# Second product of a ConvGLU as seven block products over all of K, with resident weights

## The chip, the cores and the metric

One core of one Trainium2 chip runs the kernel. The metric is the device time of one execution in microseconds; lower is better. Five engines work side by side and are told apart in the profile: TensorE (PE, its weight loads PEld), VectorE (DVE), ScalarE (ACT), GpSimd (POOL), and SyncE (SP), whose queue issues nearly all of the transfers.

## The reference

A causal decoder trunk of two layers over 1024 positions of width 1024: a hybrid attention layer and a latent attention layer, each followed by a gated MLP (ConvGLU) and a gated per-layer embedding (`ple`). The change concerns the MLP, which is the same in both layers:

```python
def conv_glu(hn, w_in, conv_w, conv_b, w_out):
    u, gate_in = jnp.split(hn @ w_in, 2, axis=-1)
    c = (conv_w[0] * shift_right(gate_in, 2) + conv_w[1] * shift_right(gate_in, 1)
         + conv_w[2] * gate_in + conv_b)
    return (jax.nn.gelu(c, approximate=False) * u) @ w_out
...
h = h + conv_glu(rmsnorm(h, ffn_norm[i]), ffn_w_in[i], ffn_conv_w[i], ffn_conv_b[i], ffn_w_out[i])
```

Everything is in 32-bit floats.

## The kernel before, in words

Activations lie transposed: features on the 128 partitions (tiles of 128, `KD` = 8 for the width, `NFT` = 22 for the MLP), positions along the free dimension in two blocks of 512 (`BW`). A product keeps 32-bit accuracy by splitting each operand into a high part and a rest (`split`, L199 to L203: ScalarE casts the high part, L202; GpSimd or VectorE subtracts it from the operand, L203) and multiplying three times, high by high, high by rest and rest by high (`mm3`, L221 to L228). So every block product is three matmuls of 128x512 for each tile of K, all of them recorded at L228.

`conv_glu` (L515) has two phases, called once per layer.

The first, `ffn_in` (L619), makes the gated activations. It already uses a seven-product scheme: for a pair of feature tiles, a 2x2 block product (two halves of K by two output tiles, two halves of K by two position blocks) is made from seven products of sums and differences of blocks (`seven`, L418; for the first pair `seven_first`, L480) where the plain way takes eight. `pair(i)` (L634) makes the four gate blocks, convolves them (`conv`, L645), makes the four up blocks, multiplies them by the gate (`up`, L656 to L661) and stores each of the four results `u` to `md` in device memory, one DMA of 256 KB each (L661). The weights pass through a ring of eight raw tiles (`raw`) and are summed on GpSimd and split on GpSimd and VectorE (`seven_weights`, L387). The seven operands of the phase are made beforehand; two of them lie in the ring of block tiles `mh`/`ml` (`block_tile`, L352, eight of each), five in a pool `x7`.

The second, `ffn_out` (L694), multiplies the activations by `w_out`, 2816 to 1024, in the plain way. `h` was put away in `hs` during the start of the MLP and is first reloaded, 16 blocks of 256 KB (L525 to L528). Then K is taken in eleven groups of two tiles. For a group the activations are loaded (`mraw`, L705) and split into `mh`/`ml`, the weights loaded (`wraw`, three buffers) and split into `whi`/`wlo` (six buffers), and for each of the 8 output tiles and 2 position blocks six matmuls go into a bank of PSUM, which VectorE then adds into `h`:

```python
for f in range(KD):
    for b in range(NBLK):
        ps = pm.tile([P, BW], F32, name="mm")
        self.mm3(ps, [((w[f // 4][0][:, f % 4], w[f // 4][1][:, f % 4]), (mh[b], ml[b]))
                      for w, (mh, ml) in zip(ws, ms)])
        nc.vector.tensor_tensor(out=h[:, f, bs], in0=h[:, f, bs], in1=ps, op=OP.add)
```

PSUM has eight banks for these products. After the MLP `ple` (L719) loads `praw`, splits it, multiplies it, norms and splits all of `h`, and multiplies again.

The kernel is written as a sequence of tile operations; the order of each engine's instructions is set by a scheduler at build time, which may put an operation ahead of others that stand before it in the text. Each engine then takes its instructions strictly in that order, and SP its transfers in its own. Memory is given out by pools: a tile that takes the place of an earlier one waits until that one has been read for the last time.

Of the kernel before, what the change touches and what calls it, by code (L numbers as in the profile page):

```python
# [11 lines left out]
F32 = mybir.dt.float32  # L12
R = mybir.dt.float32r
# [7 lines left out]
P = 128  # L21
S = 1024
# [100 lines left out]
class Trunk:  # L123
# [391 lines left out]
    def conv_glu(self, h, layer, c_h, c_raw, start):  # L515

        nc, tc, t = self.nc, self.tc, self.t
        md = [tc.dram_tile([P, S], F32, name=f"md{layer}_{i}") for i in range(NFT)]
        hs = start[0]
        with ExitStack() as ctx:  # L520
            self.ffn_in(ctx, h, layer, c_h, md, start[1])
        c_raw.close()
        pool = Lines(c_h.enter_context(tc.tile_pool(reuse_waits="tile", name=f"h2_{layer}", bufs=1, side="right")))
        h = Rows([pool.tile([P, 2, S], F32, name=f"h2_{k}") for k in range(0, KD, 2)])
        for k in range(KD):  # L525
            for b in range(NBLK):
                bs = slice(b * BW, (b + 1) * BW)
                nc.sync.dma_start(out=h[:, k, bs], in_=hs[:, k, bs])  # L528
        with ExitStack() as ctx:
            self.ffn_out(ctx, h, layer, md)  # L530
        return h
# [87 lines left out]
    def ffn_in(self, ctx, h, layer, c_h, md, operands):  # L619
# [14 lines left out]
        def pair(i):  # L634
# [5 lines left out]
            cs = [[None, None], [None, None]]  # L640

# [14 lines left out]
            def up(m, b):  # L656
                def ev(ps, add):
                    u = ep.tile([P, BW], F32, name="u", bufs=4)
                    nc.vector.tensor_tensor(out=u, in0=ps, in1=add, op=OP.add)
                    nc.vector.tensor_tensor(out=u, in0=u, in1=cs[m][b], op=OP.mult)  # L660
                    nc.sync.dma_start(out=md[tiles[m]][:, b * BW:(b + 1) * BW], in_=u)  # L661
                return ev

            outs = lambda f: [[f(m, b) for b in range(2)] for m in range(2)]
            if i == 0:
# [14 lines left out]
                for _ in ups:  # L680
                    pass
                return
# [5 lines left out]
            for _ in self.seven(ep, xs, weights(tiles), outs(up)):  # L688
                pass

# [3 lines left out]
    def ffn_out(self, ctx, h, layer, md):  # L694
        nc, tc, t = self.nc, self.tc, self.t
        wp, pm = self.wp, self.pm
        mp = Lines(ctx.enter_context(tc.tile_pool(reuse_waits="tile", name="mraw", bufs=6)))
        group = 2
        for c in range(NFT // group):
            ms, ws = [], []  # L700
            for i in range(c * group, (c + 1) * group):
                mh, ml = [[self.block_tile(j, R) for b in range(NBLK)] for j in range(2)]
                for b in range(NBLK):
                    raw = mp.tile([P, BW], F32, name="mraw")
                    nc.sync.dma_start(out=raw, in_=md[i][:, b * BW:(b + 1) * BW])  # L705
                    self.split(mh[b], ml[b], raw, eng=None if c else nc.vector)
                ms.append((mh, ml))
                src = t["ffn_w_out"][layer, i * P:(i + 1) * P, :].rearrange("p (f m) -> p f m", m=P)
                ws.append([self.weights(wp, src[:, f:f + 4], 4, P) for f in (0, 4)])
            for f in range(KD):  # L710
                for b in range(NBLK):
                    bs = slice(b * BW, (b + 1) * BW)
                    ps = pm.tile([P, BW], F32, name="mm")
                    self.mm3(ps, [((w[f // 4][0][:, f % 4], w[f // 4][1][:, f % 4]), (mh[b], ml[b]))
                                  for w, (mh, ml) in zip(ws, ms)])
                    nc.vector.tensor_tensor(out=h[:, f, bs], in0=h[:, f, bs], in1=ps, op=OP.add)  # L716
# [1150 lines left out]
def layout(inputs):  # L1867
# [6 lines left out]
    a["ffn_w_out"] = g["ffn_w_out"]  # L1874
# [71 lines left out]
```

## Time and profile before

| | us |
|---|---|
| median of 3 runs | 3014.35 |
| lowest and highest run | 3010.39, 3021.18 |
| the profiled execution, its own time | 3004.87 |
| its span, first to last instruction | 3003.2 |

The profile is of one execution. Busy time of an engine is the time in which at least one of its instructions runs; matmuls overlap, so their spacing and not their duration tells what one costs. In a row of a group, the number after the bar is the mean duration in ns, and after the second bar stands the idle time of the engine before those instructions, with what ended it. In a window's row the clock is the granted one, as a share of full speed.

### The profile page before, as it was taken

Reading aid. Unit: us, or ns where it says so; the run is one execution under the profiler, and the core shown is the slowest. Engines: PE = TensorE matmul, PEld = TensorE weight load, DVE = VectorE, ACT = ScalarE, POOL = GpSimd, SP = SyncE. Lnnn points to the kernel's source line nnn. Section 1 sums busy time; section 2 is a strip of 40 time slices with the busy share of each in tenths; the row PEclk is TensorE's granted clock in tenths of the full one; section 3 lists DMA queues with packets and bytes.
Section 4 is the critical chain, followed back from the end, with each engine's and each line's share of the span. In section 5 each row is a group of like instructions: output and inputs, shape, how many; then the busy total and the mean of one; then the engine's idle time right before and its main releaser. Section 6 shows DMA issues by size and latency. Waiting matters only on the chain.

```text
span 3003.2 us, 40819 instructions
## 1 busy us (share of the span) xinstructions
PE 2884.8 (96%) x14542; PEld 2234.5 (74%) x14542; DVE 2082.0 (69%) x3202; ACT 1259.8 (42%) x2277; POOL 1038.2 (35%) x804
## 2 busy tenths in 40 slices
PE   8999999999899999999998899999989999999997
PEld 6777777677678888888886656566758888878886
DVE  7766657875787777655798677776497777655577
ACT  6424436562343333312644434344344333422274
POOL 4332420103544444544232500010434444454323
PEclk9999989999999999999999899999989999999998
DMA  4344565635122222532121300013212222343111
GB/s 142 111 148 130 153 202 153 162 96 179 39 75 84 85 85 71 200 102 78 50 90 57 111 19 24 18 41 105 76 48 88 81 84 85 111 167 95 55 58 57
DMA packets 221020, 286.10 MB, mean 95 GB/s; under 512 B 62256, under 2 KB 106800, under 8 KB 220816
## 3 DMA queue, kind: packets, MB, share of 16 engines
q1 hardware_dynamic: 215632, 272.99, 29.3%
q10 hardware_dynamic: 5184, 10.49, 1.0%
q8 instruction: 115, 1.88, 0.3%
q14 instruction: 89, 0.73, 0.1%
HBM read 200.50 MB, written 81.79 MB: 94 GB/s over the span
## 4 chain that ended last, share of the span: by engine, by line
PE 81%; DVE 11%; issue 4%; ACT 2%; POOL 1%; DMA 1%; SPq 0%; DVEq 0%; ACTq 0%; POOLq 0%
PE mm L228 60%; PE o L1024 3%; PE s L1035 2%; PE o L1772 1%; PE tr L1760 1%; PE s L1038 1%; PE mm L995 1%; PE s L1039 1%; PE z L1744 1%; PE z L1741 1%; DVE itmp L1481 1%; PE pk L1452 1%; DVE xinv L1483 1%; DVE x L203 1%; PE mm L1059 1%
## 5 line engine op out<-in xcount | busy, mean ns | idle before, releaser
L228 PE MATMUL mm<-x,whi 128*128 128x512 f32 x1760 | 555.8, 396 | 27.0 <-DVE x L203 14.5
L203 POOL TENSOR_TENSOR wlo<-wraw,whi 128x512 fp32r<-128x512 f32 (+2 forms) x238 | 317.4, 1341 | 570.7 <-ACT whi L202 524.9
L228 PE MATMUL mm<-mh,whi 128*128 128x512 f32 x1056 | 412.9, 391 | 4.5 <-DVE h L716 4.5
L228 PEld LDWEIGHTS mm<-x,whi 128*128 128x128 f32 x1760 | 335.2, 191 | 108.4 <-DVE x L203 22.0
L228 PE MATMUL mm<-ml,whi 128*128 128x512 f32 x1056 | 413.5, 392 | 1.6 <-DVE ml L203 1.4
L228 PE MATMUL mm<-mh,wlo 128*128 128x512 f32 x1056 | 412.3, 390 | 0.0
L228 PE MATMUL mm<-xh,whi 128*128 128x512 f32 (+1 forms) x1016 | 404.8, 398 | 6.6 <-ACT xh L208 6.5
L228 PE MATMUL mm<-xh,wlo 128*128 128x512 f32 (+1 forms) x1016 | 397.3, 391 | 1.2 <-POOL wlo L203 1.2
L716 DVE TENSOR_TENSOR h<-h,mm 128x512 f32<-128x512 f32 x352 | 241.6, 687 | 220.4 <-PE mm L228 199.0
L228 PE MATMUL mm<-xl,whi 128*128 128x512 f32 (+1 forms) x1016 | 390.6, 392 | 0.5 <-DVE xl L209 0.5
L228 PE MATMUL mm<-x,wlo 128*128 128x512 f32 x880 | 346.0, 395 | 1.1 <-DVE wlo L203 1.1
L202 ACT CAST whi<-raw 128x512 fp32r<-128x512 f32 x268 | 166.3, 621 | 347.0 <-PE mm L228 305.4
L202 ACT CAST whi<-wraw 128x512 fp32r<-128x512 f32 (+2 forms) x242 | 143.0, 595 | 326.1 <-issue 147.3
L203 POOL TENSOR_TENSOR wlo<-raw,whi 128x512 fp32r<-128x512 f32 x108 | 160.7, 1489 | 301.6 <-ACT whi L202 287.1
L228 PEld LDWEIGHTS mm<-mh,whi 128*128 128x128 f32 x1056 | 199.1, 189 | 47.4 <-DVE h L716 5.4
L228 PEld LDWEIGHTS mm<-ml,whi 128*128 128x128 f32 x1056 | 199.0, 188 | 45.4 <-DVE ml L203 3.1
L228 PEld LDWEIGHTS mm<-xh,whi 128*128 128x128 f32 x1016 | 194.7, 192 | 50.7 <-ACT xh L208 7.3
L228 PEld LDWEIGHTS mm<-mh,wlo 128*128 128x128 f32 x1056 | 198.9, 188 | 41.5 <-issue 0.5
L228 PEld LDWEIGHTS mm<-xl,whi 128*128 128x128 f32 x1016 | 194.3, 191 | 44.5 <-issue 4.8
L228 PEld LDWEIGHTS mm<-xh,wlo 128*128 128x128 f32 x1016 | 194.3, 191 | 42.3 <-POOL wlo L203 2.1
L228 PEld LDWEIGHTS mm<-x,wlo 128*128 128x128 f32 x880 | 168.5, 191 | 37.2 <-DVE wlo L203 2.6
L1041 ACT ACTIVATE w<-s 128x512 f32<-128x512 f32 (+1 forms) x192 | 94.1, 491 | 166.8 <-PE s L1039 149.3
(418 smaller groups left out, 5269.0 us busy)
## 6 DMA issues: line engine op xcount, KB each, us to landing
raw<-in_ffn_w_in SPq DMA_DIRECT2D x176, 256.0 KB
wraw<-in_ffn_w_out SPq DMA_DIRECT2D x88, 256.0 KB
md<-u SPq DMA_DIRECT2D x88, 256.0 KB
mraw<-md SPq DMA_DIRECT2D x88, 256.0 KB
wraw<-in_hyb_w_in SPq DMA_DIRECT2D x52, 256.0 KB
hs<-h SPq DMA_DIRECT2D x32, 256.0 KB
h<-hs SPq DMA_DIRECT2D x32, 256.0 KB
wraw<-in_ple_w_gate SPq DMA_DIRECT2D x32, 256.0 KB
```

What stands on the lines that cost most here:

```text
L202: nc.scalar.copy(out=hi, in_=src)
L203: (eng or nc.gpsimd).tensor_tensor(out=lo, in0=src, in1=hi, op=OP.subtract)
L228: nc.tensor.matmul(ps, lhsT=w, rhs=x, start=first and i == 0, stop=last and i == len(seq) - 1)
L716: nc.vector.tensor_tensor(out=h[:, f, bs], in0=h[:, f, bs], in1=ps, op=OP.add)
L995: nc.tensor.matmul(ps[:, :n], lhsT=qh[e][0:96, i * P:(i + 1) * P], rhs=kh[ki[e]][0:96, c * BW:c * BW + n], start=True, stop=True)
L1024: nc.tensor.matmul(op_[64 * e:64 * e + 64, off:], lhsT=v[:, j, vc:vc + 64], rhs=ws[e][:, :n], start=j == 0, stop=j == nj - 1)
L1035: nc.tensor.matmul(s[:, :n], lhsT=kh[ki[e]][0:97, js], rhs=qh[e][0:97, qs], start=True, stop=False)
L1038: nc.tensor.matmul(s[:, :n], lhsT=kh[ki[e]][0:96, js], rhs=ql[e][0:96, qs], start=False, stop=False)
L1039: nc.tensor.matmul(s[:, :n], lhsT=kl[ki[e]][0:96, js], rhs=qh[e][0:96, qs], start=False, stop=True)
L1041: nc.scalar.activation(out=w[:, :n], in_=s[:, :n], func=AF.Exp, scale=MLA_SCALE)
L1059: nc.tensor.matmul(den[64 * e:64 * e + 64], lhsT=self.ones[:, :64], rhs=acc[e], start=True, stop=True)
L1452: nc.tensor.matmul(ps[:, c], lhsT=bk[rows, c0 + c, e:e + 2].rearrange("p a t -> p (a t)"), rhs=ar[rows, :, ts], start=True, stop=True)
```

## The change

`ffn_out` makes its product in the manner of `ffn_in`: K is halved by taking the two tiles of a pair as the two halves, the 1024 output features are halved into even and odd tiles, the positions into the two blocks. Each of seven jobs runs over all eleven pairs (`N`) and sums the product of one operand block and one weight block in four PSUM banks (`Q` = 4 output tiles); 33 matmuls go into each bank. The activations' seven operands are made in the first phase: three are blocks as they are (jobs 0, 1, 6), four are sums and differences, made in place on VectorE at the end of each pair (`combine`), and all seven are stored to `md`. The raw weights stay in memory for the whole phase, 44 tiles `a` of 256 KB, and GpSimd sums them in place, job after job. In a step, the operand block is loaded (into a `wraw` buffer) and split on ScalarE and VectorE, and the job's weight block is split on ScalarE and, in jobs 0 to 2, GpSimd, later VectorE. At the end of a job ScalarE copies (jobs 0, 2, 3) or VectorE adds the four banks into quarters of `h`; after jobs 3, 4 and 5 the kept `h` is loaded from `hs` through three buffers (`kept`) and added, in place of the reload at the start. `layout` brings `w_out` into the order of the blocks on the host.

```diff
@@ -515,19 +515,16 @@
     def conv_glu(self, h, layer, c_h, c_raw, start):
         nc, tc, t = self.nc, self.tc, self.t
-        md = [tc.dram_tile([P, S], F32, name=f"md{layer}_{i}") for i in range(NFT)]
+        md = [[tc.dram_tile([P, BW], F32, name=f"md{layer}_{n}_{i}") for i in range(NFT // 2)] for n in range(7)]
         hs = start[0]
         with ExitStack() as ctx:
             self.ffn_in(ctx, h, layer, c_h, md, start[1])
         c_raw.close()
         pool = Lines(c_h.enter_context(tc.tile_pool(reuse_waits="tile", name=f"h2_{layer}", bufs=1, side="right")))
         h = Rows([pool.tile([P, 2, S], F32, name=f"h2_{k}") for k in range(0, KD, 2)])
-        for k in range(KD):
-            for b in range(NBLK):
-                bs = slice(b * BW, (b + 1) * BW)
-                nc.sync.dma_start(out=h[:, k, bs], in_=hs[:, k, bs])
         with ExitStack() as ctx:
-            self.ffn_out(ctx, h, layer, md)
+            self.ffn_out(ctx, h, hs, layer, md)
         return h
     def ffn_start(self, h, layer):
@@ -638,6 +635,23 @@
                 gts.append(ep.tile([P, 2 + S], F32, name=f"gt{m}"))
                 nc.vector.memset(gts[m][:, 0:2], 0.0)
             cs = [[None, None], [None, None]]
+            us = {}
+            def store(n, x):
+                nc.sync.dma_start(out=md[n][i], in_=x)
+            def combine():
+                tt = nc.vector.tensor_tensor
+                b11, b12, b21, b22 = us[0, 0], us[0, 1], us[1, 0], us[1, 1]
+                tt(out=b22, in0=b22, in1=b12, op=OP.subtract)
+                store(5, b22)
+                tt(out=b12, in0=b12, in1=b11, op=OP.subtract)
+                store(3, b12)
+                tt(out=b11, in0=b22, in1=b11, op=OP.add)
+                store(4, b11)
+                tt(out=b21, in0=b21, in1=b11, op=OP.subtract)
+                store(2, b21)
             def gate(m, b):
                 return lambda ps, add: nc.vector.tensor_tensor(out=gts[m][:, 2 + b * BW:2 + (b + 1) * BW], in0=ps, in1=add, op=OP.add)
@@ -658,7 +672,10 @@
                     u = ep.tile([P, BW], F32, name="u", bufs=4)
                     nc.vector.tensor_tensor(out=u, in0=ps, in1=add, op=OP.add)
                     nc.vector.tensor_tensor(out=u, in0=u, in1=cs[m][b], op=OP.mult)
-                    nc.sync.dma_start(out=md[tiles[m]][:, b * BW:(b + 1) * BW], in_=u)
+                    us[m, b] = u
+                    n = {(0, 0): 0, (1, 0): 1, (1, 1): 6}.get((m, b))
+                    if n is not None:
+                        store(n, u)
                 return ev
             outs = lambda f: [[f(m, b) for b in range(2)] for m in range(2)]
@@ -679,6 +696,7 @@
                 conv(1, 1)
                 for _ in ups:
                     pass
+                combine()
                 return
             for _ in self.seven(ep, xs, weights([NFT + f for f in tiles]), outs(gate)):
                 pass
@@ -687,33 +705,83 @@
                     conv(m, b)
             for _ in self.seven(ep, xs, weights(tiles), outs(up)):
                 pass
+            combine()
         for i in range(NFT // 2):
             pair(i)
-    def ffn_out(self, ctx, h, layer, md):
+    def ffn_out(self, ctx, h, hs, layer, md):
         nc, tc, t = self.nc, self.tc, self.t
         wp, pm = self.wp, self.pm
-        mp = Lines(ctx.enter_context(tc.tile_pool(reuse_waits="tile", name="mraw", bufs=6)))
-        group = 2
-        for c in range(NFT // group):
-            ms, ws = [], []
-            for i in range(c * group, (c + 1) * group):
-                mh, ml = [[self.block_tile(j, R) for b in range(NBLK)] for j in range(2)]
-                for b in range(NBLK):
-                    raw = mp.tile([P, BW], F32, name="mraw")
-                    nc.sync.dma_start(out=raw, in_=md[i][:, b * BW:(b + 1) * BW])
-                    self.split(mh[b], ml[b], raw, eng=None if c else nc.vector)
-                ms.append((mh, ml))
-                src = t["ffn_w_out"][layer, i * P:(i + 1) * P, :].rearrange("p (f m) -> p f m", m=P)
-                ws.append([self.weights(wp, src[:, f:f + 4], 4, P) for f in (0, 4)])
-            for f in range(KD):
-                for b in range(NBLK):
-                    bs = slice(b * BW, (b + 1) * BW)
-                    ps = pm.tile([P, BW], F32, name="mm")
-                    self.mm3(ps, [((w[f // 4][0][:, f % 4], w[f // 4][1][:, f % 4]), (mh[b], ml[b]))
-                                  for w, (mh, ml) in zip(ws, ms)])
-                    nc.vector.tensor_tensor(out=h[:, f, bs], in0=h[:, f, bs], in1=ps, op=OP.add)
+        Q, N = KD // 2, NFT // 2
+        lo, hi = slice(0, BW), slice(BW, S)
+        ap = Lines(ctx.enter_context(tc.tile_pool(reuse_waits="tile", name="wout", bufs=1)))
+        kp = Lines(ctx.enter_context(tc.tile_pool(reuse_waits="tile", name="kept", bufs=3)))
+        a = [[[ap.tile([P, Q, P], F32, name=f"a{m}{k}_{i}") for k in range(2)] for m in range(2)] for i in range(N)]
+        add = lambda out, x, y: nc.vector.tensor_tensor(out=out, in0=x, in1=y, op=OP.add)
+        def load(m, k):
+            def at(i):
+                nc.sync.dma_start(out=a[i][m][k], in_=t["ffn_w_out"][layer, i, k, m])
+                return a[i][m][k]
+            return at
+        def sums(m, k, one, two, op):
+            def at(i):
+                nc.gpsimd.tensor_tensor(out=a[i][m][k], in0=a[i][one[0]][one[1]], in1=a[i][two[0]][two[1]], op=op)
+                return a[i][m][k]
+            return at
+        def s1(i):
+            load(1, 0)(i)
+            return sums(1, 0, (1, 0), (1, 1), OP.add)(i)
+        jobs = [load(0, 0), load(0, 1), load(1, 1), s1, sums(0, 0, (1, 0), (0, 0), OP.subtract),
+                sums(1, 1, (1, 1), (0, 0), OP.subtract), sums(0, 1, (0, 1), (0, 0), OP.subtract)]
+        def kept(f, bs):
+            x = kp.tile([P, BW], F32, name="kept")
+            nc.sync.dma_start(out=x, in_=hs[:, f, bs])
+            add(h[:, f, bs], h[:, f, bs], x)
+        for n, weight in enumerate(jobs):
+            ps = [pm.tile([P, BW], F32, name="mm") for q in range(Q)]
+            for i in range(N):
+                raw = wp.tile([P, BW], F32, name="wraw", bufs=self.wbufs[0])
+                nc.sync.dma_start(out=raw, in_=md[n][i])
+                xh, xl = [self.block_tile(j, R) for j in range(2)]
+                self.split(xh, xl, raw, eng=nc.vector)
+                wh, wl = [wp.tile([P, Q, P], R, name="w" + x, bufs=self.wbufs[1]) for x in ("hi", "lo")]
+                self.split(wh, wl, weight(i), eng=nc.vector if n > 2 else nc.gpsimd)
+                for q in range(Q):
+                    self.mm3(ps[q], [((wh[:, q], wl[:, q]), (xh, xl))], first=i == 0, last=i == N - 1)
+            for q in range(Q):
+                h00, h01, h10, h11 = [h[:, 2 * q + m, bs] for m in range(2) for bs in (lo, hi)]
+                if n == 0:
+                    nc.scalar.copy(out=h01, in_=ps[q])
+                elif n == 1:
+                    add(h00, ps[q], h01)
+                elif n == 2:
+                    nc.scalar.copy(out=h10, in_=ps[q])
+                elif n == 3:
+                    nc.scalar.copy(out=h11, in_=ps[q])
+                    kept(2 * q, lo)
+                elif n == 4:
+                    add(h01, ps[q], h01)
+                    add(h10, h10, h01)
+                    add(h11, h11, h01)
+                    nc.vector.tensor_copy(out=h01, in_=h11)
+                    kept(2 * q, hi)
+                elif n == 5:
+                    add(h10, ps[q], h10)
+                    add(h11, ps[q], h11)
+                    kept(2 * q + 1, lo)
+                    kept(2 * q + 1, hi)
+                else:
+                    add(h01, ps[q], h01)
     def ple(self, h, layer, last=(None, None), cuts=()):
@@ -1871,7 +1939,8 @@
     a["x"] = np.ascontiguousarray(g["x"][0].T.reshape(KD, P, S).transpose(1, 0, 2))
     a["p"] = np.ascontiguousarray(g["p"][:, 0].transpose(0, 2, 1).reshape(2, 2, P, S).transpose(0, 2, 1, 3))
     a["ffn_w_in"] = np.stack([_blocks(w) for w in g["ffn_w_in"]])
-    a["ffn_w_out"] = g["ffn_w_out"]
+    a["ffn_w_out"] = np.ascontiguousarray(g["ffn_w_out"].reshape(2, NFT // 2, 2, P, KD // 2, 2, P).transpose(0, 1, 2, 5, 3, 4, 6))
     a["ple_w_proj"] = np.stack([_blocks(w) for w in g["ple_w_proj"]])
     a["ple_w_gate"] = np.stack([_blocks(w) for w in g["ple_w_gate"]])
     cols = np.zeros((P, NCOLS), np.float32)
```

## Rows read from the trace of the kernel before

**Rows 1.** The page, part 1 (busy us by engine) and part 2 (busy tenths, clock).
```profile
PE 2884.8 (96%) x14542; PEld 2234.5 (74%) x14542; DVE 2082.0 (69%) x3202; ACT 1259.8 (42%) x2277; POOL 1038.2 (35%) x804
...
PE   8999999999899999999998899999989999999997
...
PEclk9999989999999999999999899999989999999998
```

**Rows 2.** Windows: length, PE, PEld, DVE, ACT, POOL busy us (instructions), clock, DMA share, GB/s.
```profile
860.00:1210.00 350.00, 350.00 (x1546) 289.82 (x1545) 250.13 (x354) 139.52 (x225) 159.35 (x109) 1.00 0.25 82
2660.00:2800.00 140.00, 140.00 (x619) 115.93 (x618) 70.74 (x104) 30.79 (x54) 67.65 (x54) 1.00 0.32 99
```

**Rows 3.** Timeline of TensorE around the second phase: start us, duration, operation.
```profile
1224.58 0.39 PE L228 MATMUL mm<-mh,whi 128*128 128x512 f32 x1
...
1465.97 0.39 PE L228 MATMUL mm<-mh,wlo 128*128 128x512 f32 x1
1466.20 0.39 PE L228 MATMUL mm<-ph,whi 128*128 128x512 f32 x1
```

**Rows 4.** Waits of TensorE, 800:1500, then 2200:3003: total us, times, longest.
```profile
PE mm L228 <- DVE h L716: 2.0, 1, 2.0
...
PE mm L228 <- DVE wlo L203: 0.6, 1, 0.6
...
PE mm L228 <- DVE h L716: 2.6, 1, 2.6
```

**Rows 5.** Timeline of SyncE's queue at the phase's start.
```profile
1231.78 10.03 SPq L528 DMA_DIRECT2D h<-hs  x16
```

**Rows 6.** Windows again, the stretch of the reloads.
```profile
1238.00:1248.00 10.00, 10.00 (x46) 8.26 (x45) 8.88 (x14) 1.18 (x3) 0.54 (x1) 1.00 1.06 392
```

**Rows 7.** Waits of VectorE, 1225:1470.
```profile
DVE h L716 <- DMA h<-hs: 10.9, 2, 10.1
```

**Rows 8.** Groups by line, first phase, 840:1210: busy us, mean ns.
```profile
L203 DVE TENSOR_TENSOR wlo<-raw,whi 128x512 fp32r<-128x512 f32 x79 | 67.4, 855 | 6.7 <-ACT whi L202 6.7
...
L203 POOL TENSOR_TENSOR wlo<-raw,whi 128x512 fp32r<-128x512 f32 x38 | 56.2, 1479 | 106.9 <-ACT whi L202 106.9
L660 DVE TENSOR_TENSOR u<-u,c 128x512 f32<-128x512 f32 x39 | 39.9, 1024 | 0.2
...
L407 POOL TENSOR_TENSOR raw<-raw 128x512 f32<-128x512 f32 x19 | 32.3, 1702 | 1.5
...
L659 DVE TENSOR_TENSOR u<-mm,s 128x512 f32<-128x512 f32 x38 | 26.1, 687 | 13.6 <-PE mm L228 13.6
...
L429 ACT COPY s<-mm 128x512 f32<-128x512 f32 x20 | 11.6, 580 | 0.6 <-DVE u L659 0.6
```

**Rows 9.** Groups by line, second phase, 1225:1445.
```profile
L203 POOL TENSOR_TENSOR wlo<-wraw,whi 128x512 fp32r<-128x512 f32 x40 | 51.2, 1291 | 41.0 <-ACT whi L202 41.0
...
L202 ACT CAST mh<-mraw 128x512 fp32r<-128x512 f32 x36 | 22.3, 621 | 75.9 <-PE mm L228 75.3
```

**Rows 10.** The tile `praw`: ns min/median/max, first and last start us.
```profile
L728 SPq DMA_DIRECT2D praw<-in_p x8: 328/430/511, 1244.2 to 2649.3; - x8
...
L203 POOL TENSOR_TENSOR pl<-praw,ph x8: 1288/1296/1300, 1255.0 to 2655.6; 128x512 fp32r<-128x512 f32 x8
```

**Rows 11.** Timeline of VectorE, first phase, 904:907.5.
```profile
905.38 0.75 DVE L650 SCALAR_TENSOR_TENSOR c<-gt,cols,c 128x512 f32<-128x512 f32 x1
906.04 0.68 DVE L203 TENSOR_TENSOR wlo<-raw,whi 128x512 fp32r<-128x512 f32 x1
906.64 0.74 DVE L652 SCALAR_TENSOR_TENSOR c<-gt,cols,c 128x512 f32<-128x512 f32 x1
```

**Rows 12.** Timeline of VectorE, 908:923.
```profile
915.90 0.68 DVE L660 TENSOR_TENSOR u<-u,c 128x512 f32<-128x512 f32 x1
...
919.04 1.78 DVE L660 TENSOR_TENSOR u<-u,c 128x512 f32<-128x512 f32 x1
```

**Rows 13.** Timeline of GpSimd, 908:923.
```profile
918.65 1.62 POOL L407 TENSOR_TENSOR raw<-raw 128x512 f32<-128x512 f32 x1
```

## The prediction

> **What bounds the kernel now.** I read the page first, for who is busy. TensorE is busy 96% of the span, VectorE 69%, GpSimd 35%, and the slices show TensorE at nine tenths or more nearly everywhere at the full granted clock [rows 1]. So the question for any edit is how many matmuls it issues, and then whether the helpers still keep up. Next, the windows over the phases that the change touches. In a steady 350 us of the first phase (`ffn_in`) TensorE is busy all of it, with 1546 matmuls, which is 0.2264 us from one to the next; VectorE is busy 250 of the 350 us. In a steady 140 us of the second phase (`ffn_out`, other layer) it is 619 matmuls, 0.2262 us each, with VectorE at half load and GpSimd a little under [rows 2]. A single matmul's 0.39 us overlaps its neighbours, so the spacing is the price, not the duration. Then the ends of the second phase in the timeline: it begins at 1224.58 and its last matmul starts at 1465.97, and the matmul behind it belongs to the next stage (`ple`), with no gap [rows 3]. TensorE's waits close the reading: the second phase loses 2.0 us in the first layer and 2.6 us in the second, both on the addition into `h` [rows 4]. That addition waited 10.1 us for `h<-hs` [rows 7], the 16 reloads that the queue issued in 10.03 us while the DMA moved 392 GB/s [rows 5, 6]. The second phase is therefore TensorE's own work plus 4.6 us.
>
> **The matmuls.** Before, a layer's second phase takes 22 tiles of K, 8 of output rows, 2 of columns, 3 matmuls each: 1056. After, it takes 7 jobs of 11 steps of 4 tiles, 3 matmuls each: 924. The shape stays 128x512, so two layers save 2 x 132 x 0.2264 = **59.8 us**, all on the path. The phase becomes 924 x 0.2264 = 209.2 us a layer, a job 29.9 us, a step 2.72 us.
>
> **The first phase gains** four two-input subtractions or additions (`combine`) and three more stores per pair of tiles. Such an operation (`u<-u,c`, L660) takes 0.68 us alone and 1.02 on average [rows 8, 12]. 44 x 1.024 = 45 us of VectorE a layer, against 100 us that it is idle in the 350 [rows 2], so about 82% load. The matmuls cover this, because six weight buffers let the splits run ahead. Should the cover fail, the nearest row is the one wait of 0.6 us of TensorE on a late `wlo` split [rows 4]: 22 pairs x 0.6 = 13 us. At the other end nothing is gained. I take 1 us. Of the stores, that of `b22` must have been read before `combine` overwrites it, with two products (5.4 us) in between; what is queued behind such a wait on VectorE is the next pair's splits, with the same slack. The queue gains 33 issues a layer, 0.33 us each, beside 386 us.
>
> **The start of the second phase.** The 16 reloads leave, and with them the 4.6 us. In come 44 weight loads into resident tiles, which stand where the first phase's operands and raw weights stood, so they are issued as those come free, in a burst, and the operand loads pass through the same queue among them. At the 0.63 us per load of the burst before [rows 5] they take 28 us. Only 22 loads (14 us) are wanted within the first job's 29.9 us. The lower end is 0; the upper end is half the burst in front of an operand that is due, 14 us a layer. I take 3 us a layer, nearest to the wait that 16 loads made: +6.
>
> **The helpers in the second phase.** ScalarE casts 154 tiles and copies 12 results, (154 x 0.62 + 12 x 0.58) [rows 8, 9] = 102 of 209 us: hidden. GpSimd does 33 splits and 44 weight sums; undisturbed a split is 1.29 us [rows 9], so 99 us, but the sums depend only on loads and on earlier jobs' splits, and can crowd into the first three jobs: 77 x 1.29 = 99 against 3 x 29.9 = 90 us, less six buffered steps (16 us). Lower end 0; upper end with the first phase's disturbed 1.48 and 1.70 us [rows 8], 33 x 1.48 + 44 x 1.70 = 124, minus 90, minus 16: 18 us a layer. I take 3 a layer, near the undisturbed row: +6. VectorE does 121 splits and 48 operations on results. After job 4 these are 20 operations (13.8 us at 0.69), after job 5 sixteen (11 us), each priced as a result read from PSUM [rows 8]; beside them the next job's 22 splits take 15 us. Together 28.8 of 29.9 us: just covered, if splits have been made ahead. I take 2 a layer: +4.
>
> Whether they are made ahead hangs on the order on each engine. The `ple` loads of `praw` are issued at 1244 and split on GpSimd from 1255, 210 us before their stage [rows 10], and a `wlo` split of the pair's second product runs ahead of a convolution step that the text has before it [rows 11]. The engines' order is not the text's, so splits of the next job can stand ahead of results that aren't ready.
>
> Where VectorE and GpSimd meet, the rows show turn-taking: `u<-u,c` starting 0.4 us into a GpSimd operation lasts 1.78 us and ends 0.55 us after it, while operations that read PSUM keep 0.69 [rows 8, 12, 13]. The Trainium skill (Advanced Engine Details and Errata, GPSIMD Details) says that the two engines share a read and a write interface, in conflict when VectorE has two SBUF inputs. By that rule a layer's second phase is the larger of 209 us and both engines' two-input work added, 201 us undisturbed; with the two engines taken as independent it is 209 as well, and the sum is the same by either until waiting lengthens the work, the last rival below.
>
> **The end.** `praw` can now be loaded only when the last job has read the weight tiles in its place, some 16 us before the phase ends, and needs 2 us of transfer, casts and splits (4 x 1.29). Hidden; if not, its 4 splits and 4 casts are exposed: 7.6 us a layer. Against that, three quarters of `h` are final before the last job, so `ple`'s norm can begin earlier. I take 0.
>
> **Sum.** -59.8 - 4.6 + 1 + 6 + 6 + 4 = -47.4 us. The profiled execution took 3004.87 us (span 3003.2), 9.5 us under the median of the three runs: 2957.5 as a profiled execution, **2967 us** beside the median 3014.35.
>
> **Rivals.** (a) Everything hides: only -64.4 is left, 2950 us. For it: the second phase before has no other wait [rows 4]. Against: after job 4 VectorE has 28.8 us of work in 29.9.
>
> (b) Transfers decide: 14 us a layer at the start and 7.6 at the end, 3014.35 - 64.4 + 43 = 2993 us. For it: 392 GB/s is already reached with a third of the loads [rows 5, 6]. Against: only 22 loads are urgent.
>
> (c) The order is the text's, so each job's results hold up the next job's splits. A boundary then costs what lies between the last matmul and the next operand: 3.1 us after job 0 (copy, two casts, a GpSimd split), 2.5 after jobs 2 and 3, 1.4 after job 1, 13.8 - 2.0 + 1.4 = 13.2 after job 4, 11.0 - 2.0 + 1.4 = 10.4 after job 5 (2.0 is the time that the first tile is ready ahead). That is 33.1 a layer, 66 in all: 3016 us, no change. Against it: the orders of [rows 10, 11].
>
> (d) The other side: VectorE and GpSimd taking turns become the bound of the second phase, from the point where their two-input work passes 209 us a layer. With undisturbed durations it is (121 + 28) x 0.68 + 77 x 1.29 = 201 us, just short. With those of the first phase it is 121 x 0.86 + 28 x 1.02 + 124 = 256, which is 47 us over, 94 in two layers: 3014 - 64 + 94 = 3044 us. For it: the long ones of [rows 12]. Against: the disturbed durations count the same waiting on both engines, and the first phase ran without a TensorE stall at 250 us of VectorE and 159 of GpSimd in 350 [rows 2]. The rule of the Trainium skill (Advanced Engine Details and Errata, GPSIMD Details) that was weighed above says the same of the port, and gives no duration.
>
> That the change doesn't do what it says would mean 1056 matmuls in the phase still; the loop bounds leave no room for it, so it has no chance of its own.
>
> **How the numbers follow.** Forecast 0.58; (a) 0.15; (b) 0.12; (c) 0.07; (d) 0.08. The first three are faster by over 0.3% (9 us, about what a measurement of this kernel can tell from no change): 0.85. (c) is no change, 0.07; (d) slower, 0.08. The range takes in the forecast's bounds, (a) and (b): from 2946 (2950 less the 4 us by which the lowest run lies under the median) to 3003, leaving out (c) and (d).
>
> **What would show it.** Right: 924 matmuls of 0.226 us spacing in about 209 to 217 us a layer, TensorE's waits there under 10 us, two-input VectorE operations lengthened while GpSimd is busy, and the first phase as long as before. The start is wrong if TensorE waits for a `wraw` or `a` load for more than a few us; the helpers, if it waits on `wlo` from GpSimd in jobs 0 to 2 or from VectorE in jobs 4 to 6; (c), if six gaps lie 30 us apart. The prediction falls if the second phase takes over 230 us a layer, or the first grows by more than 5 us.

## The result and the profile after

The changed kernel takes 3033.89 us (median of 5 runs, 3032.98 to 3034.89) against 3014.35 before: a ratio of 1.0064, interval 1.0047 to 1.0081. It is 0.64% slower, where 1.6% faster was forecast. The profiled execution has a span of 3031.7 us, 28.5 more than before. The page's part 1, to read against [rows 1]:

```profile
PE 2864.9 (94%) x14278; PEld 2208.4 (73%) x14278; DVE 2174.3 (72%) x3268; ACT 1339.5 (44%) x2433; POOL 1044.1 (34%) x790
```

TensorE has the 264 matmuls fewer (14278 against 14542) and is busy 20 us less, in a longer span. The windows show where the rest went (layer 0: a steady stretch of the first phase; then, in the second, two windows that hold about jobs 0 and 1, the 52 us that follow, which are the last step of job 1 and the first half of job 2, and two windows of what comes after; columns as in [rows 2]):

```profile
864.00:1214.00 350.00, 350.00 (x1546) 289.82 (x1545) 284.49 (x395) 139.64 (x227) 159.89 (x109) 1.00 0.31 104
1233.50:1263.00 29.50, 29.47 (x120) 24.00 (x121) 9.75 (x9) 13.07 (x23) 20.39 (x15) 0.92 0.86 294
1263.00:1293.00 30.00, 30.00 (x134) 24.82 (x134) 12.39 (x11) 14.54 (x27) 22.50 (x16) 1.00 0.88 301
1293.00:1345.00 52.00, 30.89 (x80) 21.99 (x79) 18.28 (x15) 7.97 (x14) 51.76 (x39) 0.70 0.20 56
1345.00:1375.00 30.00, 30.00 (x134) 24.84 (x133) 21.93 (x23) 14.53 (x26) 13.08 (x9) 1.00 0.33 97
1375.00:1465.00 90.00, 90.00 (x398) 74.51 (x397) 61.63 (x101) 39.75 (x70) 0.00 (x0) 1.00 0.39 114
```

The first phase is as before: 350 us busy in 350, the same 1546 matmuls [rows 2], VectorE up from 250 to 284. In the second, the first window holds 120 matmuls in 29.5 us and the next 134 in 30. Then 52 us hold only 80 matmuls, at a mean granted clock of 0.70 (a mix of the two levels, 1.2 and 2.4 GHz), while GpSimd is busy 51.76 of the 52. After it everything runs at full pace, and from 1375 on GpSimd does nothing at all. The ends of the phase in TensorE's timeline, as in [rows 3]:

```profile
1228.58 0.39 PE L228 MATMUL mm<-x,wlo 128*128 128x512 f32 x1
1233.53 0.80 PE L228 MATMUL mm<-mh,whi 128*128 128x512 f32 x1 [4.57 <-ACT whi L202]
...
1479.52 0.39 PE L228 MATMUL mm<-ph,whi 128*128 128x512 f32 x1
```

It begins 4.95 us after the last matmul of the first phase and lasts from 1233.53 to 1479.52, 246.0 us, against 241.6 before and the 209.2 of its matmuls. TensorE's waits (whole span, then layer 0 alone):

```profile
PE mm L228 <- POOL wlo L203: 43.4, 14, 5.0
...
PE mm L228 <- POOL wlo L203: 21.1, 6, 5.0
PE mm L228 <- ACT whi L202: 4.6, 1, 4.6
```

These replace the two waits on `h` of [rows 4]: six waits in a row on GpSimd's weight splits in layer 0, as many in layer 1, and one at the start of each phase. GpSimd's timeline has the reason (`a<-a` is a weight sum, `wlo<-a` a split):

```profile
1271.93 1.30 POOL L203 TENSOR_TENSOR wlo<-a,whi 128x512 fp32r<-128x512 f32 x1 [1.42 <-ACT whi L202]
1275.69 1.29 POOL L733 TENSOR_TENSOR a<-a,a 128x512 f32<-128x512 f32 x1 [2.46 <-DMA a<-in_ffn_w_out]
1276.94 1.29 POOL L203 TENSOR_TENSOR wlo<-a,whi 128x512 fp32r<-128x512 f32 x1
1278.19 7.65 POOL L733 TENSOR_TENSOR a<-a,a 128x512 f32<-128x512 f32 x5
1285.81 1.28 POOL L203 TENSOR_TENSOR wlo<-a,whi 128x512 fp32r<-128x512 f32 x1
1287.05 8.90 POOL L733 TENSOR_TENSOR a<-a,a 128x512 f32<-128x512 f32 x6
1295.92 1.26 POOL L203 TENSOR_TENSOR wlo<-a,whi 128x512 fp32r<-128x512 f32 x1
1297.13 6.66 POOL L733 TENSOR_TENSOR a<-a,a 128x512 f32<-128x512 f32 x5
```

Before 1272 it makes a split every 2.72 us, one per step, with pauses. Then the last weight blocks land and five or six sums stand between two splits: a split comes every 9 to 10 us. TensorE eats one split per step. The steps made ahead carry it to 1293; from the last step of job 1 to the fifth of job 2 it waits six times. The groups of those 52 us:

```profile
L733 POOL TENSOR_TENSOR a<-a,a 128x512 f32<-128x512 f32 x31 | 42.2, 1387 | 0.2
L228 PE MATMUL mm<-mh,wlo 128*128 128x512 f32 x27 | 15.9, 589 | 21.1 <-POOL wlo L203 21.1
...
L203 POOL TENSOR_TENSOR wlo<-a,whi 128x512 fp32r<-128x512 f32 x8 | 11.5, 1432 | 0.0
L203 DVE TENSOR_TENSOR ml<-wraw,mh 128x512 fp32r<-128x512 f32 x7 | 9.8, 1395 | 28.2 <-ACT mh L202 28.0
```

31 sums and 8 splits fill the stretch. TensorE idles 21.1 us in front of the matmuls that read `wlo`. 80 matmuls at 0.2264 us are 18.1 us, so 33.9 of 52 are lost: 21.1 by waiting, and the other 12.8 in matmuls that take longer (mean duration 589 ns in the group shown, in place of about 390). Most of that is the lower clock after the gaps: soon after each restart the matmuls follow one another by 0.43 us (at 1307.10, 1307.52 and 1307.95, for one) in place of 0.23.

From the landmarks in TensorE's timelines the span's 28.5 us divide so, each rounded by itself: the stage ahead of layer 0's first phase +4.0 (792.2 to 796.2); the first phases +0.3 and -0.1; the gaps at the start of the second phases +4.7 and +4.1; the second phases +4.4 and +4.2; the stretch between the layers +4.9; the tail +2.2.

### The profile page after: what moved, and what is told of

It reads as the page before. It is cut to its first block, busy times and chain, and to the rows that moved or that the text cites. A ratio compares the mean times of both kernels' runs of the same rounds, so it can differ in the third digit from the quotient of the medians.

```text
span 3031.7 us, 40726 instructions
## 1 busy us (share of the span) xinstructions
PE 2864.9 (94%) x14278; PEld 2208.4 (73%) x14278; DVE 2174.3 (72%) x3268; ACT 1339.5 (44%) x2433; POOL 1044.1 (34%) x790
## 5 line engine op out<-in xcount | busy, mean ns | idle before, releaser
L228 PE MATMUL mm<-mh,wlo 128*128 128x512 f32 x968 | 390.8, 404 | 42.2 <-POOL wlo L203 42.2
L203 POOL TENSOR_TENSOR wlo<-wraw,whi 128x512 fp32r<-128x512 f32 (+2 forms) x150 | 206.4, 1381 | 623.3 <-ACT whi L202 614.9
L228 PE MATMUL mm<-mh,whi 128*128 128x512 f32 x968 | 390.1, 403 | 8.5 <-ACT whi L202 8.5
L228 PE MATMUL mm<-ml,whi 128*128 128x512 f32 x968 | 389.9, 403 | 1.6 <-DVE ml L203 1.4
L228 PEld LDWEIGHTS mm<-mh,wlo 128*128 128x128 f32 x968 | 188.6, 195 | 90.1 <-POOL wlo L203 50.2
L203 DVE TENSOR_TENSOR ml<-wraw,mh 128x512 fp32r<-128x512 f32 x154 | 138.8, 904 | 140.3 <-ACT mh L202 140.0
L228 PEld LDWEIGHTS mm<-mh,whi 128*128 128x128 f32 x968 | 189.1, 195 | 49.4 <-ACT whi L202 9.4
L228 PEld LDWEIGHTS mm<-ml,whi 128*128 128x128 f32 x968 | 189.2, 196 | 44.6 <-DVE ml L203 3.1
L202 ACT CAST whi<-a 128x512 fp32r<-128x512 f32 x154 | 95.2, 622 | 273.8 <-PE mm L228 221.3
```

Of the source, the lines that this page charges most:

```text
L202: nc.scalar.copy(out=hi, in_=src)
L203: (eng or nc.gpsimd).tensor_tensor(out=lo, in0=src, in1=hi, op=OP.subtract)
L228: nc.tensor.matmul(ps, lhsT=w, rhs=x, start=first and i == 0, stop=last and i == len(seq) - 1)
```

## The experiments

All were timed in three rounds beside runs of the kernel before on the same chip. "Second phase" is layer 0's, from its first matmul to the first one of `ple`; "gap" is the time from the last matmul of the first phase to it, both read from TensorE's timeline. Ratios are to the kernel before.

| kernel | us | ratio (interval) | gap | second phase |
|---|---|---|---|---|
| before | 3014.35 | 1 | 0.2 | 241.6 |
| after | 3033.89 | 1.0064 (1.0047 to 1.0081) | 5.0 | 246.0 |
| e1, job 2's splits on VectorE | 2982.07 | 0.991 (0.9888 to 0.9932) | 4.4 | 222.9 |
| e2, sums behind the splits | 2975.53 | 0.988 (0.9857 to 0.9903) | 4.5 | 216.2 |
| e3, e2 and weights on ScalarE's queue | 2974.54 | 0.9885 (0.9866 to 0.9903) | 4.2 | 216.8 |
| e4, all splits on VectorE | 2980.25 | 0.9901 (0.9874 to 0.9927) | 3.9 | 220.6 |
| e5, e2 and three weights ahead | 2974.24 | 0.9877 (0.986 to 0.9894) | 0.2 | 220.0 |
| e6, e2 without the sums | 2967.0 | 0.9851 (0.982 to 0.9882) | 4.0 | 212.2 |
| e7, early weight loads | 3017.55 | 1.0015 (1.0004 to 1.0026) | 6.8 | 237.7 |
| e8, e2 and places by job | 2978.99 | 0.9891 (0.9864 to 0.9918) | 3.7 | 216.5 |
| e9, e5 and the last stores on GpSimd's queue | 2970.65 | 0.9866 (0.9842 to 0.989) | 0.2 | 216.0 |
| e10, e2 and the last stores on GpSimd's queue | 2978.01 | 0.9888 (0.9866 to 0.991) | 4.4 | 218.6 |

But for e7, the intervals of the experiments nearly all overlap one another. What tells these kernels apart below is TensorE's timeline in one profiled execution of each, of layer 0 unless layer 1 is named.

**Is it GpSimd's order?** e1 changes the engine of eleven splits:

```diff
-                self.split(wh, wl, weight(i), eng=nc.vector if n > 2 else nc.gpsimd)
+                self.split(wh, wl, weight(i), eng=nc.vector if n > 1 else nc.gpsimd)
```

> Theory (GpSimd's 44 weight sums stand ahead of job 2's splits in its queue; TensorE waits for the splits): with job 2's splits on VectorE no wait of TensorE on GpSimd is left, the second phase falls from 246 to about 212 us a layer, the whole to 3034 - 68 = 2966 us. Rival (VectorE and GpSimd take turns at two-input work, and this is the bound): GpSimd still makes its sums back to back for some 57 us while VectorE has two splits a step; each split then waits and the pair takes over 2.72 us, so part of the gain moves into waits on VectorE, 14 us a layer or more: 2994 us or later. Rival (the weight loads come too late): nothing changes, 3034 us.

Measured 2982.07 us, 51.8 less than after. TensorE's waits in layer 0:

```profile
PE mm L228 <- POOL wlo L203: 6.3, 2, 5.8
PE mm L228 <- ACT whi L202: 4.0, 1, 4.0
PE mm L228 <- DVE wlo L203: 1.8, 5, 0.4
```

Of the six waits on GpSimd one is left, 5.8 us for the last split of job 1, which still stands behind six sums; with 0.5 us at the phase's first step that is 6.3 in place of 21.1. The kernel came out 16 us above the theory's 2966. e2 keeps work and engines and changes only the order on GpSimd's queue:

```diff
         def s1(i):
             load(1, 0)(i)
-            return sums(1, 0, (1, 0), (1, 1), OP.add)(i)
+            with tc.issue_after(pooled[-1]):
+                return sums(1, 0, (1, 0), (1, 1), OP.add)(i)
...
+                if n == 2:
+                    pooled.append(last.ins if hasattr(last, "ins") else last)
```

`last` is the subtraction of the split; the edge is on the order of issue only.

> The same work on the same engines; only the order of GpSimd's queue differs: the first sum of each pair is issued behind the last split of job 2. Theory (order): no wait on GpSimd in job 2; 212 us a layer, 2966 us, or some us more where job 3 waits for its first sums. Rival (taking turns): the sums crowd into job 3, where VectorE has two splits a step; the jam moves there and the time is 2990 us or later. Rival (late loads): 3034 us.

Measured 2975.53 us, 58.4 less than after, with the same instructions. No wait on GpSimd is left:

```profile
PE mm L228 <- ACT whi L762: 4.1, 1, 4.1
PE mm L228 <- DVE wlo L763: 2.3, 6, 0.7
```

```profile
1236.40:1452.50 216.10, 213.75 (x924) 174.47 (x925) 168.21 (x168) 100.54 (x177) 128.08 (x85) 0.99 0.51 163
```

The last row is the window over the whole second phase: 924 matmuls in 216 us, the clock at 0.99. That the order of one queue cost some 30 us a layer is shown by this pair (246.0 against 216.2 us in layer 0, 246.4 against 215.5 in layer 1). e4, on the changed kernel, moves all splits to VectorE:

```diff
-                self.split(wh, wl, weight(i), eng=nc.vector if n > 2 else nc.gpsimd)
+                self.split(wh, wl, weight(i), eng=nc.vector)
```

> All weight splits of the second phase on VectorE, so that GpSimd only sums. Theory (order): as with job 2's alone on VectorE, 2966 us. Rival (taking turns): two splits a step on VectorE throughout; same price as with job 2 alone, since the sums fall into the same stretch, 2990 us or later. If VectorE's order puts results behind later splits, waits appear at the ends of jobs 0 to 2 that the other kernel lacks.

Measured 2980.25. VectorE, with two splits a step beside the sums, fell behind in jobs 2 and 3 (ten waits on `wlo`, 5.3 us, the longest 2.0); the phase is 4.4 us longer than in e2 and 2.3 shorter than in e1. No wait at the ends of jobs stands out from those of the steps beside it.

**What does the taking of turns cost?** In e2 the sums run beside VectorE's two splits a step. VectorE's and GpSimd's timelines 139 us into the phase:

```profile
1375.59 1.77 DVE L203 TENSOR_TENSOR ml<-wraw,mh 128x512 fp32r<-128x512 f32 x1
1377.28 1.77 DVE L763 TENSOR_TENSOR wlo<-a,whi 128x512 fp32r<-128x512 f32 x1
1378.98 1.77 DVE L203 TENSOR_TENSOR ml<-wraw,mh 128x512 fp32r<-128x512 f32 x1
```

```profile
1375.08 10.22 POOL L733 TENSOR_TENSOR a<-a,a 128x512 f32<-128x512 f32 x6
```

Each split lasts 1.77 us in place of 0.68, one sum of 1.7 us passes between two of them, and a step takes 3.40 us in place of 2.72: TensorE waits six times for such a split, 2.3 us in all. e6 is e2 with the line of `sums` that adds or subtracts left out (jobs 3 to 6 take the raw blocks, so 44 sums a layer are not computed):

```diff
-                nc.gpsimd.tensor_tensor(out=a[i][m][k], in0=a[i][one[0]][one[1]], in1=a[i][two[0]][two[1]], op=op)
```

> As the kernel with the sums behind the splits, but the 44 weight sums a layer on GpSimd are left out (jobs 3 to 6 use the raw blocks). Price of taking turns, taken alone: VectorE's splits should return from about 0.9 to 0.68 us, the run of 3.4 us steps in jobs 3 and 4 and its waits on wlo should vanish, the phase fall from 216 to about 212 us a layer: 2967 us. If the waits stay, they are VectorE's own load (splits and results) and not GpSimd's.

Measured 2967.0 us and a second phase of 212.2 us, as expected. The groups of 1360:1420, first in e2, then in e6 (the operands' splits; the weights' are alike), and TensorE's waits of the phase in e6:

```profile
L733 POOL TENSOR_TENSOR a<-a,a 128x512 f32<-128x512 f32 x17 | 28.9, 1737 | 0.0
L203 DVE TENSOR_TENSOR ml<-wraw,mh 128x512 fp32r<-128x512 f32 x24 | 26.3, 1094 | 2.2 <-ACT mh L202 2.1
L763 DVE TENSOR_TENSOR wlo<-a,whi 128x512 fp32r<-128x512 f32 x23 | 25.5, 1110 | 0.0
```

```profile
L203 DVE TENSOR_TENSOR ml<-wraw,mh 128x512 fp32r<-128x512 f32 x20 | 13.7, 686 | 1.5 <-ACT mh L202 1.5
```

```profile
PE mm L228 <- ACT whi L761: 3.6, 1, 3.6
```

VectorE's splits go from 1.1 us back to 0.69 and all waits on it vanish: the turns cost 4.0 us in layer 0 and 3.2 in layer 1 (215.5 to 212.3), and VectorE's own load nothing.

**Was it the late loads?** The 44 loads of `a` in the changed kernel, from its first to its last issue (us from the start):

```profile
L727 SPq DMA_DIRECT2D a<-in_ffn_w_out x44: 376/430/1716, 1229.5 to 1282.7; - x44
```

They take 53 us, and those that the sums need come last. e7 puts them first in the changed kernel:

```diff
-            load(1, 0)(i)
             return sums(1, 0, (1, 0), (1, 1), OP.add)(i)
...
-        jobs = [load(0, 0), load(0, 1), load(1, 1), s1,
+        jobs = [first, load(0, 1), lambda i: a[i][1][1], s1,
```

`first(i)` loads blocks (1, 1), (1, 0) and (0, 0) of pair `i`.

> The changed kernel with its engines as they are; the blocks of job 2 and 3 are loaded right beside those of job 0, so that the sums can begin in job 0 and don't all come after the last loads. Theory (late loads made the 44 sums crowd into one job, which is why the loss was 34 us a layer and not the 18 of the estimate): the sums spread over jobs 0 and 1, two beside each split, 3 x 1.29 = 3.9 us against a step of 2.72; 18 us a layer or less is lost, 2990 to 3004 us. Rival (the loss is the same work whenever it comes): about 3034 us.

Measured 3017.55 us, 16 less than after, and less gained than expected. GpSimd's timeline and the groups of the first 120 us of the phase:

```profile
1252.40 1.26 POOL L203 TENSOR_TENSOR wlo<-a,whi 128x512 fp32r<-128x512 f32 x1
1253.74 2.88 POOL L733 TENSOR_TENSOR a<-a,a 128x512 f32<-128x512 f32 x2
1256.58 1.26 POOL L203 TENSOR_TENSOR wlo<-a,whi 128x512 fp32r<-128x512 f32 x1
```

```profile
L733 POOL TENSOR_TENSOR a<-a,a 128x512 f32<-128x512 f32 x43 | 60.9, 1423 | 3.9 <-DMA a<-in_ffn_w_out 1.4
L228 PE MATMUL mm<-mh,wlo 128*128 128x512 f32 x135 | 57.7, 428 | 13.1 <-POOL wlo L203 12.6
...
L203 POOL TENSOR_TENSOR wlo<-a,whi 128x512 fp32r<-128x512 f32 x33 | 51.8, 1568 | 2.2 <-ACT whi L202 2.2
```

Two sums stand between two splits, which come every 4.18 us against a step of 2.72. 43 sums and 33 splits are 112.7 us of the 120; the 405 matmuls of the stretch are worth 91.7, so 28 us are lost. Late loads made the jam steeper (33.9 us in 52), but it is there without them; and the gap at the start grew to 6.8 us. The prediction's upper end of 18 had taken off 16 us for buffered steps; here the sums begin at the start of the phase, when none have been made.

**What makes the gap at the start?** SyncE's queue in the changed kernel, where TensorE's last matmul of the first phase stands at 1228.58:

```profile
1229.16 0.32 SPq L641 DMA_DIRECT2D md<-u  x1
1229.53 1.39 SPq L727 DMA_DIRECT2D a<-in_ffn_w_out  x3
1231.22 2.64 SPq L641 DMA_DIRECT2D md<-u  x4
1233.95 4.46 SPq L727 DMA_DIRECT2D a<-in_ffn_w_out  x8
```

The first three weight loads are issued behind the store at 1229.16, the fourth behind four stores that wait for `combine`. e3 is e2 with job 0's loads on ScalarE's queue:

```diff
-                nc.sync.dma_start(out=a[i][m][k], in_=t["ffn_w_out"][layer, i, k, m])
+                (nc.sync if m or k else nc.scalar).dma_start(out=a[i][m][k], in_=t["ffn_w_out"][layer, i, k, m])
```

> As the kernel with the sums behind the splits, and job 0's eleven weight loads go out on ScalarE's queue. Theory (the 4.9 and 4.3 us gaps at the start come from SyncE's order: the first weight load stands behind the stores of the last pair): the gaps fall under 1 us each, some 9 us less than the kernel with the sums behind the splits. Rival (the weights' places are free only then): no difference. Rival (the DMA engines are the limit in the burst): the gaps move into the first steps, no difference.

Measured 2974.54, the gap 4.2: no difference, but ScalarE's order had four loads ahead of its first cast of a weight, and two of them were issued only from 1231.6 on, so the gap itself doesn't separate order from place. One thing it does show: its first two loads went out at 1226.51 and 1226.92, 3 us ahead of the first phase's last matmul (1229.82), so the places of these two tiles were free by then. e8 is e2 with the resident tiles laid out job by job and not pair by pair:

```diff
-        a = [[[ap.tile([P, Q, P], F32, name=f"a{m}{k}_{i}") for k in range(2)] for m in range(2)] for i in range(N)]
+        b = {(m, k, i): ap.tile([P, Q, P], F32, name=f"a{m}{k}_{i}") for m, k in ((0, 0), (0, 1), (1, 1), (1, 0)) for i in range(N)}
+        a = [[[b[m, k, i] for k in range(2)] for m in range(2)] for i in range(N)]
```

> As the kernel with the sums behind the splits; the weight tiles are laid out job by job, so that the first eight blocks of job 0 lie where the raw weights of the first phase lay, which are read for the last time well before its end. Theory (places): the first loads find their place free early and the gap of 4.4 us goes, about 5 us a layer less, 2966 us. Rival (SyncE's order holds them: they stand behind the store of the last pair's b21): the gap stays, 2975 us.

Measured 2978.99, gap 3.7: a store still stood in the queue right ahead of the first load, which went out 0.2 us after the first phase's last matmul, in place of 0.9 in e2. e5 is e2 with the first three blocks loaded once more, into the `wraw` ring:

```diff
                 x = weight(i)
+                if n == 0 and i < 3:
+                    x = wp.tile([P, Q, P], F32, name="wraw", bufs=self.wbufs[0])
+                    nc.sync.dma_start(out=x, in_=t["ffn_w_out"][layer, i, 0, 0])
```

> As the kernel with the sums behind the splits; in addition the first three weight blocks of job 0 are loaded once more into the wraw ring, which is free during the first phase, and split from there. Theory (the gap of 4.4 us at the start of each second phase comes from weight tiles whose places come free only with the first phase's last products): the gap falls under 1 us, and half-clock steps after it go too, some 4 to 6 us a layer: about 2966 us against 2975.5. Rival (the queue's order and the stores before it): the gap stays.

Measured 2974.24: the gap went (0.2), and a wait of 4.6 us came at the fourth step, so phase and gap together took 220.2 us against 220.7 in e2. The fourth block's load is the first in the third row:

```profile
1232.78 1.45 SPq L727 DMA_DIRECT2D a<-in_ffn_w_out  x3
1235.07 2.98 SPq L641 DMA_DIRECT2D md<-u  x4
1238.13 1.07 SPq L727 DMA_DIRECT2D a<-in_ffn_w_out  x2
```

It stands behind the four stores of `combine`. e9 (on e5) and e10 (on e2) send the last pair's stores, all but the first, to GpSimd's queue:

```diff
-                nc.sync.dma_start(out=md[n][i], in_=x)
+                (nc.gpsimd if i == NFT // 2 - 1 and n else nc.sync).dma_start(out=md[n][i], in_=x)
```

> The kernel with the first three weights loaded ahead; the stores of the last pair other than the first go out on GpSimd's queue, so that no weight load of the second phase stands behind them on SyncE's. Theory (order of the queue): neither the gap at the start nor its successor at the fourth step appears; about 5 us a layer less than 2974 us, 2964 us. Rival (the places come free only with the last products, and the loads need 3 to 4 us from there): the gap at the fourth step stays over 2 us.

> The kernel with the sums behind the splits, and only the stores of the last pair moved to GpSimd's queue, without the weights loaded ahead. Theory (order of the queue alone): the gap at the start falls from 4.4 to under 1 us. Rival (places): it stays near 4 us, since the first weight load waits for TensorE's last reads.

TensorE's waits on ScalarE's cast of the weights in the phase, first e9, then e10:

```profile
PE mm L228 <- ACT whi L765: 1.2, 1, 1.2
```

```profile
PE mm L228 <- ACT whi L762: 4.0, 1, 4.0
```

With the stores alone the wait stays at 4.0 us. SyncE's queue and ScalarE's first cast of a weight in e10, whose first phase ends with a matmul at 1229.48:

```profile
1228.18 0.92 SPq L757 DMA_DIRECT2D wraw<-md  x2
1229.15 4.97 SPq L727 DMA_DIRECT2D a<-in_ffn_w_out  x9
```

```profile
1233.17 0.62 ACT L762 CAST whi<-a 128x512 fp32r<-128x512 f32 x1 [6.16 <-DMA a<-in_ffn_w_out]
```

The loads now go out without a pause, but behind operand loads that wait for VectorE's splits (3.6 us in three waits), and the first block is cast 4.0 us after its load was issued. So the gap here is a load that is issued only as the first phase ends. That the places of the tiles hold the loads is not shown, and for the first two blocks e3 speaks against it. With the stores moved and three blocks ahead (e9) the fourth block's load goes out 3.1 us after the first phase's last matmul in place of 7.5 (e5), and the wait falls from 4.6 us to 1.2. Gap and phase together fall from 220.2 (e5) to 216.2 us in layer 0, but only from 219.2 to 218.0 in layer 1. e9 came out at 2970.65 us, 1.3% under the kernel before.

## Why the prediction was wrong

**The matmuls** were right: 924 a layer at 0.226 us, 14278 in all, and in e6 the phase is 212.2 us, 3.0 above their 209.2.

**The first phase** was right: +0.3 and -0.1 us where 1 us was taken, VectorE at 81% (284 of 350) where 82% was said.

**The helpers in the second phase** is the step that failed, in the sentence on GpSimd: "Lower end 0; upper end ... 18 us a layer. I take 3 a layer, near the undisturbed row". The mechanism was named, the sums crowding ahead of the splits, but as a load and not as an order. The prediction's own signs for it came: TensorE waits on `wlo` from GpSimd, and the phase takes over 230 us. Measured: 33.9 us in layer 0, above the upper end, for two reasons. 40 of the 44 sums crowded into 70 us, from 1276 to 1345, and not into the 90 us of three jobs, as the last weight loads were issued only near 1283; the steps made ahead were used up by 1293, and behind them each split came 7 to 10 us after the one before. And TensorE's clock fell with the gaps: that is most of the 12.8 us beyond the waits, for which the sum had no term at all. Layer 1 shows the same six waits and 21.1 us. Twice 30.9 us too little is 62 us. The forecast missed by 66.9 us beside the medians, and by 76 by the profiled executions (3033.79 against 2957.5); the rest of these 76 is 8 us more at the start than the 6 taken and 11 us outside the two phases, less some 5 us taken for VectorE and the first phase that did not come.

**The start** was set too low: 3 us a layer, measured 4.7 and 4.1 beyond the gap before, plus a clock of 0.92 in the first 29.5 us (120 matmuls are worth 27.2, so 2.3 us). "Half the burst in front of an operand" was not it: the loads were late because they were issued only at the end of the first phase, behind its stores and the operand loads.

**VectorE after jobs 4 and 5** was covered, as argued: 2 us a layer were taken for it, and nothing was lost there; TensorE is busy all 90 us from 1375 to 1465, in which jobs 3, 4 and 5 end.

**The rivals.** (a), that everything hides, did not come either: 33.9 us of layer 0's phase lay open. (c), the text's order, is refuted: no gaps at the ends of jobs. The scheduler's freedom, which spoke against (c), did the harm: it put sums that no one needed for 30 us ahead of splits that were due. (d) named the side on which it fell, and its mechanism is there (splits at 1.77 us), but it is not the bound: 3.2 to 4.0 us a layer, where its case had 47. The Trainium skill (Advanced Engine Details and Errata, GPSIMD Details) says that the two engines share a read and a write interface and conflict when VectorE has two SBUF inputs. The trace agrees: 1.1 us a split beside GpSimd's sums in e2, 0.69 without them in e6. (b) was partly right in kind, as the start was late, but not in size (14 us a layer), and its late end of the phase did not come: the first matmul of `ple` follows without a gap. With the one edit that undoes the failed step (e2) the kernel takes 2975.5 us beside a kernel before of 3011.4: 35.8 less, against 47.4 forecast.

**Left open** is what lies outside the two phases. Layer 0's first phase begins at 792.2 before, 796.2 after, 792.4 in e1 and 799.6 in e2, though no edit touches anything ahead of it. For the changed kernel the largest piece is a stretch of the attention with some 105 matmuls and no wait of TensorE: it takes 15.6 us before (444.3 to 459.9) at a granted clock of 0.75, and 21.5 us after (443.5 to 465.0) at 0.50, the lower of the two levels throughout. Other stretches give 2 us back. Why the clock rose later there is open. Between the layers the changed kernel takes 4.9 us more, and e2 as much (723.0 against 718.5); its waits on `kvn` from GpSimd are 5.0 us there against 1.5 before. No run bears on it.

## What to carry to other kernels

Where a scheduler orders each engine's queue, work that is ready early and needed late, on an engine that also has work due now, is a hazard even if the engine's total load fits (GpSimd was busy 34% of the span here): look at who stands behind it in the queue, and pin the order or split the engines. Price a late operand on TensorE at its wait plus the slower matmuls after it, here 21.1 + 12.8 us. And weights whose loads stand in the queue behind the last phase's stores and operand loads begin to come when that phase ends, so the first steps need operands that were loaded before (gap 0.2 us in e5).

## What the runs showed of the hardware that was not expected

With GpSimd summing without a pause, VectorE's two-input operations settled at exactly one GpSimd operation each: 1.77 us against 0.68, 1.70 apart, step after step, so two splits made a step of 3.40 us whatever TensorE wanted.

The Trainium skill (DMA: Bandwidth & Descriptors, Issuing engines are not separate DMA queues) says that starting transfers from several engines only saves the issuing engine's time. Here the queue's order mattered beside its time: with three weights ahead, moving six stores to GpSimd's queue let the fourth weight load go out 4.4 us earlier against the end of the first phase, because it no longer stood behind stores whose data weren't ready, and TensorE's wait fell from 4.6 us (e5) to 1.2 (e9).
